# A recurrent mixer with both directions' gates and scans merged, on one core of Trainium2

## The chip, the cores and the metric

The kernel runs on one core of a Trainium2 chip. The core has four compute engines with a queue of their own each: TensorE (PE; its weight loads are listed as PEld), VectorE (DVE), ScalarE (ACT) and GpSimd (POOL). A fifth, SyncE (SP), issues most of the DMA transfers. Each queue is worked off in order, and engines wait for each other by semaphores. The metric is the device time of one execution in microseconds, as the median of the runs.

## The reference

Two layers work on 256 latent tokens and 256 context tokens of width 1024, in fp32. Layer 0 is differential attention and a SwiGLU. Layer 1 is a gated linear recurrence in two directions (the part that is changed) and a mixture of eight experts of which each token takes two. Cut to the recurrence:

```python
def rglru_coeffs(u, w_gates, b_gates, a_param):
    ...
    g = jax.nn.sigmoid(g.astype(jnp.float32))
    r_t, i_t = g[0], g[1]
    log_a = RG_C * r_t * jax.nn.log_sigmoid(a_param.astype(jnp.float32))
    a_t = jnp.exp(log_a)
    b_t = jnp.sqrt(-jnp.expm1(2.0 * log_a)) * (i_t * u.astype(jnp.float32))
    return a_t, b_t

def rglru_mixer(...):
    gate_l = jax.nn.gelu(proj_l[..., :D_RNN])
    u_l = depthwise_conv(proj_l[..., D_RNN:], conv_w, conv_b)
    u_c = depthwise_conv(proj_c[..., D_RNN:], conv_w, conv_b)
    for d, reverse in enumerate((False, True)):
        a_c, b_c = rglru_coeffs(u_c, gate_w[d], gate_b[d], a_param[d])
        h_c = linear_scan(a_c, b_c, h0, reverse)
        h_c_final = h_c[:, 0] if reverse else h_c[:, -1]
        a_l, b_l = rglru_coeffs(u_l, gate_w[d], gate_b[d], a_param[d])
        lat_states.append(linear_scan(a_l, b_l, h_c_final, reverse))
    y_l = ((lat_states[0] + lat_states[1]) * gate_l) @ w_out
```

The context is scanned first and hands its last state to the scan of the latents. Behind it come the residual, a norm, the router and the experts.

## The kernel before, in words

Channels lie on the 128 partitions, so the 1024 channels are eight blocks `b` of 128 x 512 (256 latents, then 256 context tokens). Most products are made in three passes: a weight is split into a rounded half (`split_hi`, a cast on ScalarE, line 148) and a rest (`split_lo`, a subtraction on VectorE or GpSimd, line 152). `hi(key)` and `lo(key)` do that for the two halves of one load.

For each block the recurrence goes through these steps:
- `u_proj(b)` on TensorE: 24 products into a PSUM bank; `gate_proj(g)` makes the gate of two blocks, whose copy (line 1235) is on ScalarE.
- `conv(b)`: four VectorE operations (lines 1255 to 1258) from that bank into `u`.
- `gate_mm(b)`: four TensorE products `lg` (line 1265), two gates for each direction.
- `gates(b)` on ScalarE: for each direction Sigmoids into `r_t` and `i_t` (line 1274) and a Tanh into `t_t` (line 1275).
- `exps(b, own)` on ScalarE: `a = exp(...)` in place of `r_t` (line 1289) and its square into `a2`, which is another Exp (line 1288), or for directions under `own` a GpSimd product (line 1291).
- `in_gate(b)`: `i_t` times `u` (line 1279); on GpSimd for blocks 2, 6 and 7, else on VectorE. `one_less(b)` on VectorE: `(a2 + 1) * t_t` (line 1298). `roots(b)` on ScalarE: a square root of that (line 1302). All of these are done once for each direction.
- `scans(b)` on VectorE: for each direction a product (line 1308) and two scans (lines 1311 to 1317), then the sum of both directions into `YS` (line 1320). `times_gate(k0, k1)` multiplies `YS` by the gate (line 1328).

`r_t`, `i_t` and `t_t` exist four times, so `gates(4)` waits until `scans(0)` has read its tiles. ScalarE loads a table whenever it changes between Sigmoid and Tanh, Exp, Sqrt and Gelu. VectorE, ScalarE, TensorE, GpSimd and SyncE run this part in the order in which the lines 1423 to 1536 stand, an order written out by hand that mixes the steps of several blocks.

Behind it TensorE makes the output projection `acc` from `YS` (`w_out_part`, line 1569): slices 0 to 3 for four output tiles, then slices 4 and 5, then, tile by tile, slices 6 and 7 (`w_out_end`), each followed by `add_out` (lines 486 and 487) on VectorE, a sum of squares on ScalarE, transposes, the router's logits and its choice of two, and the gather of the first expert's tokens (`gather_split`, lines 1385 to 1406). Six halves of the first expert's weights are split early: `first.split(2, eng)` for GpSimd, VectorE, GpSimd (line 1583). The rest is split as the experts run, six halves ahead of TensorE (`splits_due`). The experts' weights, 1 MB a tile, go into buffers that come free as tiles of the recurrence are done and later as weights are used.

Of the kernel before, what the change touches and what calls it, by code (L numbers as in the profile page):

```python
# [9 lines left out]
F32 = mybir.dt.float32  # L10
F32R = mybir.dt.float32r
I32 = mybir.dt.int32
AF = mybir.ActivationFunctionType
OP = mybir.AluOpType
# [3 lines left out]
P = 128  # L18
D = 1024
KD = D // P  # L20
SEQ = 256
CTX = 256
NTOK = SEQ + CTX
# [68 lines left out]
V_CB = V_CW + 32  # L92
# [6 lines left out]
def body(tc, nc, cst, rope, vec, lamv, modb, fing, x, ctx, w_m0, w_mod, w_q, w_k, w_v, w_o,  # L99
         w_gu, w_dn, w_u, w_g, w_lg, w_lo, w_rt, m_gu, m_dn, out):  # L100
    mm = nc.tensor.matmul
    V, A, G = nc.vector, nc.scalar, nc.gpsimd
# [235 lines left out]
    vc = persist.tile([P, V_N], F32, name="vc")  # L338
# [159 lines left out]
    st = pool(name="start", bufs=2)  # L498
# [88 lines left out]
    with tc.manual_schedule(engines={ENG.PE, ENG.DVE, ENG.Activation, ENG.Pool}):  # L587
# [93 lines left out]
        ls = persist.tile([P, 3, 16], F32, name="ls")  # L681
# [251 lines left out]
    with tc.manual_schedule(engines={ENG.PE, ENG.DVE, ENG.Activation, ENG.Pool}):  # L933
# [9 lines left out]
        for u in range(NH * 4):  # L943
# [9 lines left out]
            if wT:  # L953
                pv(*wT)
                if qt == 0:
                    root, scale = head_norm(hd - 1)
# [30 lines left out]
        root, scale = head_norm(NH - 1)  # L987
# [155 lines left out]
    for half in range(2):  # L1143
        FHt = fp.tile([P, FH, NTOK], F32R, name="FHt", bufs=1)
        FLt = fp.tile([P, FH, NTOK], F32R, name="FLt", bufs=1)
        first = 0
        if half == 0:

            first = 2
# [73 lines left out]
    blk = {}  # L1223
# [19 lines left out]
    def u_proj(b, c0=0, c1=NTOK):  # L1243

        w, j = wus[b // 2], b % 2
        if b not in blk:
            blk[b] = {"u": US[b] if b < 4 else lru_u.tile([P, NTOK], F32, name="U"), "ps": bank("u")}
        for k in range(KD):
            mm3(blk[b]["ps"][:, c0:c1], w(k, j * P, (j + 1) * P), (hH[:, k, c0:c1], hL[:, k, c0:c1]),
                start=(k == 0), stop=(k == KD - 1))  # L1250

    def conv(b):
        u, ps = [t.rearrange("p (s t) -> p s t", s=2) for t in (blk[b]["u"], blk[b]["ps"])]
        cw = [vc[:, V_CW + q * 8 + b:V_CW + q * 8 + b + 1] for q in range(4)]
        V.tensor_scalar(u, ps, cw[2], vc[:, V_CB + b:V_CB + b + 1], op0=OP.mult, op1=OP.add)
        V.scalar_tensor_tensor(u[:, :, 2:], ps[:, :, :SEQ - 2], cw[0], u[:, :, 2:], op0=OP.mult, op1=OP.add)
        V.scalar_tensor_tensor(u[:, :, 1:], ps[:, :, :SEQ - 1], cw[1], u[:, :, 1:], op0=OP.mult, op1=OP.add)
        V.scalar_tensor_tensor(u[:, :, :SEQ - 1], ps[:, :, 1:], cw[3], u[:, :, :SEQ - 1],
                               op0=OP.mult, op1=OP.add)

    def gate_mm(b):
        blk[b]["lg"] = []
        for ds in range(4):
            ps = bank("lg")
            mm(ps, wlg[b // 4][:, b % 4, ds], blk[b]["u"], start=True, stop=True)  # L1265
            blk[b]["lg"].append(ps)

    def gates(b):
        r, it, tt = [lru.tile([P, 2, NTOK], F32, name=n, tag=f"{n}{b % 4}", bufs=1) for n in ("r_t", "i_t", "t_t")]
        blk[b].update(r=r, i=it, t=tt)  # L1270
        for d in range(2):
            for s in range(2):
                col = V_GB + (2 * d + s) * 8 + b
                A.activation((r, it)[s][:, d], blk[b]["lg"][2 * d + s], AF.Sigmoid, bias=vc[:, col:col + 1])
            A.activation(tt[:, d], r[:, d], AF.Tanh, scale=ls[:, 2, d * 8 + b:d * 8 + b + 1])

    def in_gate(b, eng=G):
        for d in range(2):
            eng.tensor_tensor(blk[b]["i"][:, d], blk[b]["i"][:, d], blk[b]["u"], op=OP.mult)

    def exps(b, own):

        r = blk[b]["r"]
        blk[b]["a2"] = []
        for d in range(2):
            a2 = lru.tile([P, NTOK], F32, name="a2", bufs=3)
            if d >= own:
                A.activation(a2, r[:, d], AF.Exp, scale=ls[:, 1, d * 8 + b:d * 8 + b + 1])
            A.activation(r[:, d], r[:, d], AF.Exp, scale=ls[:, 0, d * 8 + b:d * 8 + b + 1])
            if d < own:  # L1290
                G.tensor_tensor(a2, r[:, d], r[:, d], op=OP.mult)
            blk[b]["a2"].append(a2)

    def one_less(b):

        tt = blk[b]["t"]
        for d in range(2):
            V.scalar_tensor_tensor(tt[:, d], blk[b]["a2"][d], 1.0, tt[:, d], op0=OP.add, op1=OP.mult)

    def roots(b):  # L1300
        for d in range(2):
            A.activation(blk[b]["t"][:, d], blk[b]["t"][:, d], AF.Sqrt)

    def scans(b):
        st = []
        for d in range(2):
            aa, bv = blk[b]["r"][:, d], blk[b]["i"][:, d]
            V.tensor_mul(bv, bv, blk[b]["t"][:, d])
            s = lr2.tile([P, NTOK], F32, name=f"st{d}")
            if d == 0:  # L1310
                V.tensor_tensor_scan(s[:, SEQ:], aa[:, SEQ:], bv[:, SEQ:], 0.0, op0=OP.mult, op1=OP.add)
                V.tensor_tensor_scan(s[:, :SEQ], aa[:, :SEQ], bv[:, :SEQ], s[:, NTOK - 1:NTOK],
                                     op0=OP.mult, op1=OP.add)
            else:
                V.tensor_tensor_scan(s[:, :SEQ - 1:-1], aa[:, :SEQ - 1:-1], bv[:, :SEQ - 1:-1], 0.0,
                                     op0=OP.mult, op1=OP.add)
                V.tensor_tensor_scan(s[:, SEQ - 1::-1], aa[:, SEQ - 1::-1], bv[:, SEQ - 1::-1],
                                     s[:, SEQ:SEQ + 1], op0=OP.mult, op1=OP.add)
            st.append(s)
        V.tensor_add(YS[:, b], st[0][:, :SEQ], st[1][:, :SEQ])  # L1320
# [5 lines left out]
    def times_gate(k0, k1):  # L1326
        y, gt = [t[:, k0:k1].rearrange("p k n -> p (k n)") for t in (YS, GT)]
        V.tensor_mul(y, y, gt)
# [87 lines left out]
    with tc.manual_schedule(engines={ENG.PE, ENG.DVE, ENG.Activation, ENG.Pool, ENG.SP}):  # L1416
# [41 lines left out]
        gate_mm(2)  # L1458
        lo(("g", 1))
        exps(0, 0)  # L1460
        in_gate(0, V)
        u_proj(3)
        one_less(1)
        conv(3)
# [6 lines left out]
        one_less(2)  # L1471
        roots(0)
        load_u(3)
        in_gate(1, V)
        conv(4)
        roots(2)
        gate_mm(3)
# [17 lines left out]
        scans(1)  # L1495
        gate_mm(5)
        gates(5)
        in_gate(3, V)
        lo(("g", 3))
        exps(5, 1)  # L1500
        one_less(3)
# [5 lines left out]
        gate_proj(3)()  # L1507
        gelu(0, 8)
        one_less(5)
        scans(3)  # L1510
        roots(5)
        roots(4)
        u_proj(7)
        times_gate(0, 4)
        conv(7)
        gate_mm(6)
        in_gate(4, V)
        gate_mm(7)
        in_gate(5, V)
        scans(4)  # L1520
        gates(6)
        gates(7)
        exps(6, 0)
        scans(5)
        one_less(6)
        exps(7, 1)
        one_less(7)
        times_gate(4, 6)
        in_gate(6)
        roots(7)  # L1530
        roots(6)
        scans(6)
        in_gate(7)
        scans(7)
        times_gate(6, 7)
        times_gate(7, 8)
        close(lru_u)
        close(lru)
# [28 lines left out]
        def w_out_part(t, dh, ks):  # L1567
            for kk in ks:
                mm(acc[t, dh], YS[:, kk, t * P:(t + 1) * P], ws[dh, kk // 4][:, kk % 4], start=(kk == 0),
                   stop=(kk == KD - 1))  # L1570
# [9 lines left out]
        for tag in ("whi", "wlo"):  # L1580
            halves.put(tag, [hip.tile([P, 1024], F32R, name=tag, tag=tag) for _ in range(HL)])
        mem["hi"] = halves
        for eng in (G, V, G):
            first.split(2, eng)
        for t in range(2):
            for kk in range(4, 6):
                for dh in range(2):
                    w_out_part(t, dh, [kk])

# [56 lines left out]
            V.scalar_tensor_tensor(key[:, t], rk[:, t * NE:(t + 1) * NE], 1.0, mask[:, t], op0=OP.add, op1=OP.mult)  # L1646

        def w_out_end(t, dh):
            w_out_part(t, dh, range(6, KD))
            add_out(rt, acc[t, dh], G1b, t, dh)  # L1650

        w_out_end(0, 0)
# [528 lines left out]
```

## Time and profile before

| | |
|---|---|
| median of 3 runs | 1687.04 us (1685.44 to 1689.09) |
| the profiled execution | 1685.75 us, its span 1683.9 us |
| TensorE busy | 1636.5 us, 97% of the span |
| VectorE, ScalarE, GpSimd busy | 1100.8, 794.3, 61.3 us |
| from the first cast for the recurrence's third load to the last gating product | 679 to 798 us |
| first product of the experts | 818 us |

A profiled execution lists every instruction with its start (us from the start of the span) and length, and in brackets how long its engine had been idle before it and which instruction ended that. Busy time of TensorE is no measure of need, since its matmuls overlap; idle time of an engine matters only where that engine is the one the others wait for. The changed lines lie between 668 and 830 us, some 10% of the span. Everything behind runs in an order that the change leaves alone.

### The profile page before, as it was taken

To read this page: it belongs to the slowest core of one execution; us is meant where nothing else is said; L and a number is where in the kernel's file an instruction comes from. 1 tells how busy PE (TensorE), PEld (TensorE's weight loads), DVE (VectorE), ACT (ScalarE), POOL (GpSimd) and SP (SyncE) were. 2 spreads that over 40 slices of the span, in tenths; PEclk is the share of its full clock that TensorE was granted. 3 is DMA by queue.
4 is the path that set the end of the run, shared out by engine and by line. 5 is a ranking of instruction groups with operands and counts; after the bars stand their busy time and mean duration, and the time that the engine had idled before them with its cause. 6 is when DMAs were issued, how large, how long until landed. Compare 5 with 4: busy or idle time off the path is not lost.

```text
span 1683.9 us, 21275 instructions
## 1 busy us (share of the span) xinstructions
PE 1636.5 (97%) x7878; PEld 1154.3 (69%) x7878; DVE 1100.8 (65%) x1595; ACT 794.3 (47%) x1194; POOL 61.3 (4%) x62
## 2 busy tenths in 40 slices
PE   8999999999999999996999999999999999999996
PEld 6877788888788878772777656566565665656642
DVE  5578887967675735799797567465675665655522
ACT  4366674422122324894675455344554444544411
POOL 0001110000000001114000000000000000000000
PEclk9999999999999999998999999999999999999998
DMA  9333313545664622235888999999999999999994
GB/s 381 114 151 150 151 51 129 209 178 181 237 255 133 246 90 94 90 146 196 327 321 347 374 417 420 421 417 404 417 420 421 419 404 418 420 420 419 403 420 202
DMA packets 75488, 480.35 MB, mean 285 GB/s; under 512 B 14284, under 2 KB 14924, under 8 KB 18920
## 3 DMA queue, kind: packets, MB, share of 16 engines
q1 hardware_dynamic: 66976, 474.38, 70.5%
q10 hardware_dynamic: 8392, 4.45, 1.1%
q8 instruction: 66, 1.08, 0.3%
q14 instruction: 54, 0.44, 0.1%
HBM read 477.70 MB, written 1.10 MB: 284 GB/s over the span
## 4 chain that ended last, share of the span: by engine, by line
PE 91%; DVE 6%; ACT 1%; issue 1%; DMA 0%; POOL 0%; ACTq 0%; SPq 0%; POOLq 0%; DVEq 0%
PE b L1829 12%; PE b L332 9%; PE b L333 9%; PE b L334 9%; PE b L1880 6%; PE gu L332 5%; PE gu L333 5%; PE gu L334 5%; PE dacc L332 2%; PE dacc L333 2%; PE dacc L334 2%; PE b L1374 2%; PE p L334 1%; PE p L332 1%; PE p L333 1%; PE lg L1265 1%
## 5 line engine op out<-in xcount | busy, mean ns | idle before, releaser
L152 DVE TENSOR_TENSOR wlo<-raw,whi 128x1024 fp32r<-128x1024 f32 x341 | 405.8, 1216 | 114.0 <-ACT whi L148 112.7
L148 ACT CAST whi<-raw 128x1024 fp32r<-128x1024 f32 x346 | 352.7, 1044 | 221.2 <-PE b L333 63.8
L332 PE MATMUL b<-whi,xH 128*128 128x512 f32 x448 | 181.9, 406 | 1.2 <-ACT xH L1402 1.2
L1829 PE MATMUL b<-raw,xF 128*64 128x512 f32 x592 | 180.9, 594 | 0.0
L334 PE MATMUL b<-wlo,xH 128*128 128x512 f32 x448 | 177.6, 396 | 2.1 <-DVE wlo L152 2.1
L333 PE MATMUL b<-whi,xL 128*128 128x512 f32 x448 | 177.7, 397 | 0.0
L332 PE MATMUL gu<-hH,whi 128*128 128x512 f32 (+1 forms) x384 | 143.0, 372 | 0.0
L334 PE MATMUL gu<-hL,whi 128*128 128x512 f32 (+1 forms) x384 | 142.6, 371 | 0.0
L333 PE MATMUL gu<-hH,wlo 128*128 128x512 f32 (+1 forms) x384 | 142.6, 371 | 0.0
L152 DVE TENSOR_TENSOR wlo<-mraw,whi 128x1024 fp32r<-128x1024 f32 x106 | 126.6, 1222 | 23.4 <-ACT whi L148 23.1
L148 ACT CAST whi<-mraw 128x1024 fp32r<-128x1024 f32 x106 | 108.1, 1049 | 34.0 <-PE b L333 32.5
L1829 PE MATMUL b<-mraw,xF 128*64 128x512 f32 x304 | 118.2, 595 | 0.0
L1846 ACT ACTIVATE sges<-b 128x256 f32<-128x256 f32 x28 | 10.7, 384 | 223.0 <-PE b L1829 223.0
L1829 PEld LDWEIGHTS b<-raw,xF 128*64 128x64 f32 x592 | 55.8, 137 | 87.4 <-issue 84.1
L332 PEld LDWEIGHTS b<-whi,xH 128*128 128x128 f32 x448 | 84.3, 188 | 36.1 <-issue 16.1
L1847 DVE TENSOR_TENSOR sges<-sges,b 128x256 f32<-128x256 f32 x28 | 11.8, 421 | 145.3 <-ACT sges L1846 145.3
L1106 DVE SCALAR_TENSOR_TENSOR mac<-raw,SC,mac 128x512 f32<-128x512 f32 x140 | 98.2, 749 | 4.1 <-DMA raw<-w_mod 3.2
L334 PEld LDWEIGHTS b<-wlo,xH 128*128 128x128 f32 x448 | 84.3, 188 | 23.0 <-DVE wlo L152 2.6
L333 PEld LDWEIGHTS b<-whi,xL 128*128 128x128 f32 x448 | 84.4, 188 | 19.0 <-DVE xL L1403 0.5
L1880 PE MATMUL b<-raw,aF 128*64 128x512 f32 x352 | 91.2, 598 | 0.5 <-ACT aF L1858 0.5
L332 PE MATMUL b<-whi,aH 128*128 128x512 f32 x224 | 89.0, 397 | 0.0
L333 PE MATMUL b<-whi,aL 128*128 128x512 f32 x224 | 88.4, 395 | 0.0
(350 smaller groups left out, 2954.3 us busy)
## 6 DMA issues: line engine op xcount, KB each, us to landing
raw<-m_gu SPq DMA_DIRECT2D x147, 1024.0 KB
raw<-m_dn SPq DMA_DIRECT2D x86, 1024.0 KB
mraw<-m_gu SPq DMA_DIRECT2D x77, 1024.0 KB
raw<-w_mod SPq DMA_DIRECT2D x40, 1024.0 KB
mraw<-m_dn SPq DMA_DIRECT2D x26, 1024.0 KB
raw<-w_gu SPq DMA_DIRECT2D x22, 1024.0 KB
mw<-w_m SPq DMA_DIRECT2D x8, 1024.0 KB
raw<-w_dn SPq DMA_DIRECT2D x8, 1024.0 KB
```

The lines of the kernel that those rows point to most:

```text
L148: A.copy(h["hi"][:, :h["w"]], h["src"])
L152: eng.tensor_tensor(h["lo"][:, :h["w"]], h["src"], h["hi"][:, :h["w"]].bitcast(F32), op=OP.subtract)
L332: mm(ps, lh, rh, start=start, stop=False)
L333: mm(ps, ll, rh, start=False, stop=False)
L334: mm(ps, lh, rl, start=False, stop=stop)
L1106: V.scalar_tensor_tensor(ac[:, q], w[:, j], SC[:, k, m:m + 1], ac[:, q], op0=OP.mult, op1=OP.add)
L1265: mm(ps, wlg[b // 4][:, b % 4, ds], blk[b]["u"], start=True, stop=True)
L1374: mm(ps, XN[:, t, k * P:(k + 1) * P], oh[:, t, 0:ps.shape[-1]], start=(t == 0 and n == 0), stop=(t == 1 and n == per - 1))
L1829: mm(gu[0][64 * h:64 * h + 64], xF[:, kk], w, start=(kk == 0), stop=(kk == KD - 1), tile_position=(0, 64 * h), skip_group_check=True)
L1846: A.activation(part, ps[:, 0:256], AF.Silu)
L1847: V.tensor_mul(part, part, ps[:, 256:512])
L1880: mm(E[i]["y"][64 * dh:64 * dh + 64], lhs, w, start=(c == 0 and j == 0), stop=(c == EC - 1 and j == 3), tile_position=(0, 64 * dh), skip_g ...
```

## The change

- `conv`: the first of its four operations goes to ScalarE, as an Identity with scale and bias.
- `in_gate`, `one_less`, `roots` and the product in `scans` work on both directions in one instruction of 128 x 1024. `in_gate` is on VectorE for every block. The scans write in place of `i_t`. `a2` is two tiles of double size instead of three.
- Order: `u_proj(7)`, `conv(7)`, `gate_mm(6)` and `gate_mm(7)` go ahead of `scans(3)`; both `gates(6)` and `gates(7)` go ahead of `scans(4)`, `exps(7, 1)` ahead of `scans(5)`; `in_gate(6)` and `in_gate(7)` stand between `one_less(6)` and `scans(6)`; `times_gate(6, 7)` goes ahead of `scans(7)`.
- Four halves of the experts' weights are split early, all four on GpSimd, instead of six.
- Slice 6 of the output projection is multiplied along with slices 4 and 5; `w_out_end` only does slice 7.

```diff
-        V.tensor_scalar(u, ps, cw[2], vc[:, V_CB + b:V_CB + b + 1], op0=OP.mult, op1=OP.add)
+        A.activation(u, ps, AF.Identity, scale=cw[2], bias=vc[:, V_CB + b:V_CB + b + 1])
...
-    def in_gate(b, eng=G):
+    def in_gate(b):
+        it, u = blk[b]["i"], blk[b]["u"]
+        V.tensor_tensor(it, it, u[:, None].to_broadcast([P, 2, NTOK]), op=OP.mult)
+
+    def exps(b, own):
+
+        r = blk[b]["r"]
+        a2 = blk[b]["a2"] = lru.tile([P, 2, NTOK], F32, name="a2", bufs=2)
         for d in range(2):
-            eng.tensor_tensor(blk[b]["i"][:, d], blk[b]["i"][:, d], blk[b]["u"], op=OP.mult)
...
         tt = blk[b]["t"]
-        for d in range(2):
-            V.scalar_tensor_tensor(tt[:, d], blk[b]["a2"][d], 1.0, tt[:, d], op0=OP.add, op1=OP.mult)
+        V.scalar_tensor_tensor(tt, blk[b]["a2"], 1.0, tt, op0=OP.add, op1=OP.mult)
 
     def roots(b):
-        for d in range(2):
-            A.activation(blk[b]["t"][:, d], blk[b]["t"][:, d], AF.Sqrt)
+        A.activation(blk[b]["t"], blk[b]["t"], AF.Sqrt)
 
     def scans(b):
         st = []
+        V.tensor_mul(blk[b]["i"], blk[b]["i"], blk[b]["t"])
         for d in range(2):
             aa, bv = blk[b]["r"][:, d], blk[b]["i"][:, d]
-            V.tensor_mul(bv, bv, blk[b]["t"][:, d])
-            s = lr2.tile([P, NTOK], F32, name=f"st{d}")
+            s = bv
...
         one_less(5)
-        scans(3)
+        u_proj(7)
+        conv(7)
         roots(5)
         roots(4)
-        u_proj(7)
+        gate_mm(6)
+        gate_mm(7)
+        scans(3)
         times_gate(0, 4)
-        conv(7)
-        gate_mm(6)
-        in_gate(4, V)
-        gate_mm(7)
-        in_gate(5, V)
-        scans(4)
+        in_gate(4)
+        in_gate(5)
         gates(6)
         gates(7)
+        scans(4)
         exps(6, 0)
+        exps(7, 1)
         scans(5)
         one_less(6)
-        exps(7, 1)
+        in_gate(6)
         one_less(7)
+        roots(6)
+        roots(7)
         times_gate(4, 6)
-        in_gate(6)
-        roots(7)
-        roots(6)
+        in_gate(7)
         scans(6)
-        in_gate(7)
+        times_gate(6, 7)
         scans(7)
-        times_gate(6, 7)
         times_gate(7, 8)
...
-        for eng in (G, V, G):
-            first.split(2, eng)
-        for t in range(2):
-            for kk in range(4, 6):
+        first.split(4, G)
+        for kk in range(4, 7):
+            for t in range(2):
                 for dh in range(2):
                     w_out_part(t, dh, [kk])
...
-            w_out_part(t, dh, range(6, KD))
+            w_out_part(t, dh, [KD - 1])
```

## Rows read from the trace of the kernel before

**Rows 1.** The page, chain of work that ended last, by engine

```profile
PE 91%; DVE 6%; ACT 1%; issue 1%; DMA 0%; POOL 0%; ACTq 0%; SPq 0%; POOLq 0%; DVEq 0%
```

**Rows 2.** By stretch: us, busy us and instructions, granted clock, DMA share, GB/s

```profile
690.00:720.00 30.00, 30.00 (x129) 21.73 (x128) 21.74 (x26) 29.75 (x43) 5.01 (x4) 1.00 0.31 108
721.60:798.20 76.60, 59.36 (x228) 36.46 (x227) 74.89 (x90) 53.61 (x71) 23.11 (x13) 0.93 0.44 165
...
1000.00:1100.00 100.00, 100.00 (x467) 62.72 (x464) 60.27 (x69) 45.48 (x57) 0.00 (x0) 1.00 1.01 421
```

**Rows 3.** Timeline 676 to 690 (start, us, engine, line): ScalarE, then VectorE

```profile
679.24 1.05 ACT L148 CAST whi<-raw 128x1024 fp32r<-128x1024 f32 x1 [2.72 <-issue]
...
681.71 1.28 ACT L1274 ACT_TABLE_LOAD   x1
686.96 0.69 ACT L1274 ACTIVATE r_t<-lg,vc 128x512 f32<-128x512 f32 x1 [3.97 <-PE lg L1265]
...
686.10 0.81 DVE L1255 TENSOR_SCALAR U<-u,vc 128x512 f32<-128x512 f32 x1 [2.11 <-PE u L334]
```

**Rows 4.** Timeline of ScalarE, 667 and 716 to 723

```profile
667.09 1.11 ACT L461 ACTIVATE tp<-tp,sh,gs 128x256 f32<-128x256 f32 x2 [2.43 <-PE tp L447]
...
716.63 0.69 ACT L1274 ACTIVATE r_t<-lg,vc 128x512 f32<-128x512 f32 x1
...
722.51 2.02 ACT L148 CAST whi<-raw 128x1024 fp32r<-128x1024 f32 x2
```

**Rows 5.** Timeline of VectorE, 712 to 723

```profile
712.03 1.28 DVE L1279 TENSOR_TENSOR i_t<-i_t,U 128x512 f32<-128x512 f32 x2
...
718.58 0.81 DVE L1255 TENSOR_SCALAR U<-u,vc 128x512 f32<-128x512 f32 x1
719.42 0.75 DVE L1256 SCALAR_TENSOR_TENSOR U<-u,vc,U 128x508 f32<-128x508 f32 x1
...
721.65 0.68 DVE L1308 TENSOR_TENSOR i_t<-i_t,t_t 128x512 f32<-128x512 f32 x1
722.37 0.69 DVE L1311 TENSOR_TENSOR_SCAN st<-r_t,i_t 128x256 f32<-128x256 f32 x1
```

**Rows 6.** Timeline 768 to 794: VectorE, then GpSimd

```profile
771.91 6.56 DVE L1298 SCALAR_TENSOR_TENSOR t_t<-a,t_t 128x512 f32<-128x512 f32 x4
...
784.11 2.78 DVE L1308 TENSOR_TENSOR i_t<-i_t,t_t 128x512 f32<-128x512 f32 x1
...
772.85 6.75 POOL L1279 TENSOR_TENSOR i_t<-i_t,U 128x512 f32<-128x512 f32 x4
781.19 10.58 POOL L152 TENSOR_TENSOR wlo<-raw,whi 128x1024 fp32r<-128x1024 f32 x4 [1.59 <-ACT whi L148]
```

**Rows 7.** Timeline 735 to 803: VectorE, then TensorE

```profile
735.91 2.35 DVE L152 TENSOR_TENSOR wlo<-raw,whi 128x1024 fp32r<-128x1024 f32 x2
...
739.79 0.28 PE L332 MATMUL gp<-hH,whi 128*128 128x256 f32 x1
...
751.01 3.60 PE L1265 MATMUL lg<-U,wlg 128*128 128x512 f32 x8
760.39 5.13 PE L1265 MATMUL lg<-U,wlg 128*128 128x512 f32 x8 [5.78 <-DVE U L1258]
...
797.84 5.19 PE L1569 MATMUL acc<-wlo,YS 128*128 128x512 f32 x8 [10.51 <-DVE YS L1328]
```

**Rows 8.** Timeline 797 to 818: VectorE, ScalarE, TensorE

```profile
797.37 0.75 DVE L1328 TENSOR_TENSOR YS<-YS,GT 128x256 f32<-128x256 f32 x2
...
801.36 0.69 DVE L486 TENSOR_TENSOR xadd<-acc,G1b 128x512 f32<-128x512 f32 x1 [0.96 <-PE acc L1569]
...
808.19 0.69 DVE L487 TENSOR_TENSOR XL<-XL,xadd 128x512 f32<-128x512 f32 x1
...
816.46 0.89 ACT L1394 ACTIVATE gath<-gath,sh,gs 128x128 f32<-128x128 f32 x2 [4.75 <-PE gath L1374]
...
817.96 0.48 PE L332 MATMUL b<-whi,xH 128*128 128x512 f32 x1
```

More of the change, by code (lines that the diff above doesn't have):

```diff
@@ L1275, in gates @@
             A.activation(tt[:, d], r[:, d], AF.Tanh, scale=ls[:, 2, d * 8 + b:d * 8 + b + 1])
-    def in_gate(b, eng=G):
-        for d in range(2):
-            eng.tensor_tensor(blk[b]["i"][:, d], blk[b]["i"][:, d], blk[b]["u"], op=OP.mult)
+    def in_gate(b):
+        it, u = blk[b]["i"], blk[b]["u"]
+        V.tensor_tensor(it, it, u[:, None].to_broadcast([P, 2, NTOK]), op=OP.mult)
     def exps(b, own):
         r = blk[b]["r"]
-        blk[b]["a2"] = []
+        a2 = blk[b]["a2"] = lru.tile([P, 2, NTOK], F32, name="a2", bufs=2)
         for d in range(2):
-            a2 = lru.tile([P, NTOK], F32, name="a2", bufs=3)
             if d >= own:
-                A.activation(a2, r[:, d], AF.Exp, scale=ls[:, 1, d * 8 + b:d * 8 + b + 1])
+                A.activation(a2[:, d], r[:, d], AF.Exp, scale=ls[:, 1, d * 8 + b:d * 8 + b + 1])
             A.activation(r[:, d], r[:, d], AF.Exp, scale=ls[:, 0, d * 8 + b:d * 8 + b + 1])
             if d < own:
-                G.tensor_tensor(a2, r[:, d], r[:, d], op=OP.mult)
-            blk[b]["a2"].append(a2)
+                G.tensor_tensor(a2[:, d], r[:, d], r[:, d], op=OP.mult)
     def one_less(b):
         tt = blk[b]["t"]
-        for d in range(2):
-            V.scalar_tensor_tensor(tt[:, d], blk[b]["a2"][d], 1.0, tt[:, d], op0=OP.add, op1=OP.mult)
+        V.scalar_tensor_tensor(tt, blk[b]["a2"], 1.0, tt, op0=OP.add, op1=OP.mult)
     def roots(b):
-        for d in range(2):
-            A.activation(blk[b]["t"][:, d], blk[b]["t"][:, d], AF.Sqrt)
+        A.activation(blk[b]["t"], blk[b]["t"], AF.Sqrt)
     def scans(b):
         st = []
+        V.tensor_mul(blk[b]["i"], blk[b]["i"], blk[b]["t"])
         for d in range(2):
             aa, bv = blk[b]["r"][:, d], blk[b]["i"][:, d]
-            V.tensor_mul(bv, bv, blk[b]["t"][:, d])
-            s = lr2.tile([P, NTOK], F32, name=f"st{d}")
+            s = bv
             if d == 0:
@@ L1460, in body @@
         exps(0, 0)
-        in_gate(0, V)
+        in_gate(0)
         u_proj(3)
@@ L1473, in body @@
         load_u(3)
-        in_gate(1, V)
+        in_gate(1)
         conv(4)
@@ L1497, in body @@
         gates(5)
-        in_gate(3, V)
+        in_gate(3)
         lo(("g", 3))
```

## The prediction

> **What bounds the kernel now.** I read the page first: the chain that ended last is 91% TensorE and 6% VectorE [rows 1]. The 6% is what an edit of the recurrence can reach, so the next view is the table by stretch [rows 2]. From 690 to 720 us TensorE is busy 30.00 of 30 us and ScalarE 29.75: ScalarE has no slack there, while VectorE has 8 us. From 721.6 to 798.2 it is the other way round: VectorE is busy 74.89 of 76.6 us, which is back to back but for the gaps between dependent instructions, and TensorE only 59.36. So one loop runs through both: ScalarE sets the pace until the first scans, VectorE from there to the last gating product, which ends at 798.1 [rows 8]. TensorE then finishes the output projection, the router and the gather, and the experts' first product starts at 817.96 [rows 8]. From 1000 to 1100 us the DMA share is 1.01 [rows 2], so the loads run without a pause there. What shifts the start of the experts shifts the buffers that their loads wait for, so I carry a shift of 817.96 to the end one to one. The question is where 817.96 goes.
>
> **The change, part by part.**
>
> (a) *ScalarE's queue up to the first scans.* The first operation of `conv` moves from VectorE to ScalarE. There it stands in program order: `conv(2)` (line 1450) is ahead of the casts `hi(("u", 2))` (line 1452), which are ahead of `gates(0)`. Before, ScalarE made the first of those two casts at 679.24, loaded the table at 681.71, and then sat idle 3.97 us until the gates' products came at 686.96 [rows 3]. After, the first of these is the operation of `conv(2)`, which waits for `u_proj(2)`; VectorE's row of the same step has it start at 686.10, released by that product [rows 3]. Nothing behind it on ScalarE can use the idle time. Its price: the trace shows no such instruction on 512 columns. The nearest rows are the Sigmoid from PSUM on 512 columns, 0.69 us [rows 3], and Identity on 256 columns, 1.11 us for two [rows 4], so 0.55 each; the same step on VectorE took 0.81 [rows 5]. I take 0.69 with 0.1 of it overlapped by the next, because size and source are the same, and keep 0.55 to 0.81. So `gates(0)` starts at 686.1 + 0.6 + two casts of 0.95 + a load of 1.3 = 689.9, late by 2.9 us. ScalarE has no slack in 690 to 720 to win this back, and takes on two more such operations (`conv(3)`, `conv(4)`): 1.2 us more, less 0.2 for square roots done in three calls rather than six. `gates(3)` goes from 716.63 [rows 4] to 720.5. Behind it, in order, stand two casts and the copy of the gate projection, and only then the operation of `conv(5)`. From 716.63 to the end of that copy's slot at 722.51 are 5.9 us, so it runs at 726.4 to 727.1. VectorE stands still for it, although it could have gone on at 719.42 as before; the three other operations of `conv(5)` follow (719.42 to 721.65, 2.2 us [rows 5]), and `scans(0)` starts at 729.4 rather than 721.65: **7.7 us late**. VectorE's relief up to here is worth nothing; it only waits longer.
>
> One sentence of the Trainium skill bears on this price without entering it: the page "ScalarE: Activation LUTs", section "Table sets: the hidden batching unit", says that identity is in every table set. The trace agrees as far as it goes, since Identity at 667.09 runs with no load in front [rows 4], but no row shows it between Sigmoids or Exps. Were it not so, each of these operations could cost two loads of 1.28 us, and ScalarE would be later still.
>
> (b) *VectorE from the first scans to the last.* It works without a break, so instructions are counted.
> - First operation of `conv(6)` and `conv(7)` gone: 2 x 0.84 (718.58 to 719.42 [rows 5]) = -1.7.
> - The scans' two products in one: a 128x512 one holds its successor up by 0.72 (721.65 to 722.37 [rows 5]); a subtraction on 128x1024 lasts 1.22 (two in 2.35 [rows 7]), or 1.26 with the gap; -0.18 each, eight times: -1.4.
> - `in_gate(3)` to `in_gate(5)` and `one_less(3)` to `one_less(7)`: a pair takes 1.28 [rows 5], one of double size 1.22; -0.05 each: -0.4.
> - `in_gate(6)` and `in_gate(7)` come over from GpSimd: 2 x 1.15 = +2.3.
> - With that GpSimd's four products go, and so does their hold on VectorE. Beside them four `one_less` took 6.56 us [rows 6], against 2.4 at the pair's pace [rows 5]. -4.1 (a square of `exps(7, 1)` on GpSimd stays, and holds VectorE as now).
> - GpSimd's four weight splits stay as many. Their place in the code is behind `roots`, and what releases them is the cast on ScalarE, not the scans; the first starts some 2 us behind `one_less(7)`, so beside `scans(6)` as now. One of them and one operation of VectorE alternate: 10.58 us for four, while a product of 0.68 took 2.78 [rows 6]. Longer operations of VectorE don't change what GpSimd takes in between, about 2 us each. 0.
>
> Sum: -5.3. Against it stands a new wait. `conv(7)` now precedes `scans(3)`, and on VectorE everything queues behind it. `u_proj(7)` follows `gate_proj(3)` on TensorE, which needs the split weights of `lo(("g", 3))`. VectorE made these at 735.91, before TensorE asked at 739.79 [rows 7]; now the first is there at 735.91 + 7.7 - 0.4 + 1.2 = 744.4. TensorE idles close to 5 us. After 5.78 us of idling eight product records took 5.13 us instead of 3.60 [rows 7], so I add 1.7 for the lowered clock (0 if it holds). Projections as before 11.2 us (739.79 to 751.01 [rows 7]): 757.5, and with ScalarE's step 758.2. VectorE is there at 751.1 + 7.7 - 1.5 = 757.3. It waits about 1 us. The early `conv(7)` spares TensorE its 5.78 us wait of now, but TensorE is not what the scans wait for.
> The last gating product ends at 798.1 + 7.7 - 5.3 + 1.0 = 801.5, 3.4 us late.
>
> (c) *The tail.* Now the last two slices of the output projection are multiplied behind the scans, at the lowered clock after 10.51 us of idling: eight records in 5.19 us [rows 7]. The first addition starts at 801.36, 3.2 us behind the last gating product, and the last ends at 808.88 [rows 8], with VectorE waiting for TensorE in between. After, slice 6 is multiplied during `scans(7)` and raises the clock again, and slice 7 needs one matmul per tile: the first addition starts 1.3 us behind (-1.9), and four additions of 1.4 us with one wait for the row sums make 6.7 instead of 7.5 (-0.8). Together -2.7. Two VectorE splits (2.36 us) that now hide behind TensorE's slow start also go; they hid there, 0.
>
> (d) *The splits not made early.* Four halves are ready when the experts start, not six. Two casts and two subtractions move into the experts' first steps. ScalarE idles 4.75 us before the gathered tokens come [rows 8]; if they are queued there they are free, if they stand behind it they cost up to 2 x 1.15 = 2.3. I take 0.4, since their inputs and buffers are free long before.
>
> Sum: +3.4 - 2.7 + 0.4 = +1.1. The profiled execution took 1685.75 us, 1.3 under the median of 1687.04; it would become 1686.9, and the median **1688.1 us**. With the ends of the unknown prices (four operations at 0.55 or 0.81; no drop of the clock; 0 or 2.3 for the splits) the likeliest case reaches from 1686.2 to 1691.0.
>
> **The rivals.**
> *ScalarE keeps up.* If its new operations fell into idle time (the queue built in another order than the program's lines), `scans(0)` would start 0.8 us early, VectorE would meet `u_proj(7)` at 751.0 and wait 3.8 us there, and the scans would end at 798.1 - 1.7 - 5.3 + 3.8 = 794.9; with the tail and (d) -5.5: 1681.5. For it: the 3.97 us of idling [rows 3]. Against: every queue of the recurrence follows the lines of the program. 0.18.
> *The moved splits decide (slower).* If both engines take them ahead of the gathered tokens' scaling, the first product waits 2.3 us, and TensorE, idle that long, gets the lower clock, 1.7 us as in (b): 2.3 + 1.7 = 4.0 more than nothing, instead of 0.4: 1691.7. It decides from the point at which the fifth half is not split when TensorE is through four. For it: ScalarE and VectorE then have the scaling, the splits and their normal supply to do at once; against: ScalarE's idle time in front [rows 8]. 0.22.
> *GpSimd's splits really come behind the scans*, as the change's title says. Then the hold of 4 x 2 us on the last scans goes: 1680.1. The Trainium skill speaks for that order: "GPSIMD Engine Reference", section "8. Key points", says that the two engines contend where VectorE reads two SBUF inputs, as the scans do, and the rows above agree. But no wait puts the splits there. 0.06.
>
> **How the numbers follow.** Likeliest case 0.50, the rivals 0.18, 0.22 and 0.06, the rest open. A change under 0.2% (3.4 us) can't be told from none here: 1683.7 to 1690.4. Faster holds two rivals, 0.23; slower the second rival and the end of the likeliest case, 0.27; the same, 0.50. The range reaches from the first rival to beyond the second: 1681.0 to 1693.0.
>
> **What would show it.** Right: ScalarE casting for `u, 2` behind 686; VectorE idle for some 5 us in front of `conv(5)` with ScalarE as the releaser; `scans(0)` near 729; TensorE idle near 740 to 745; GpSimd's splits beside `scans(6)` with VectorE operations of 2.6 us; the first addition within 1.5 us of the last gating product. Wrong: `scans(0)` before 724, or the splits behind 800.

## The result: slower by 0.85%, and the profile after

| | before | after |
|---|---|---|
| median | 1687.14 us | 1702.58 us (1699.70 to 1703.08) |
| ratio | 1 | 1.0085, 95% interval 1.0073 to 1.0097 |
| span of the profiled execution | 1683.9 us | 1697.8 us |
| `scans(0)` starts | 721.65 | 729.54 (forecast 729.4) |
| last gating product ends | 798.12 | 803.23 (forecast 801.5) |
| first addition starts | 801.36 | 814.25 (forecast 802.8) |
| first product of the experts | 817.96 | 831.95 |

The forecast was 1688.1 in a range of 1681.0 to 1693.0: wrong by some 14 us. The table already says where to look. The first half of the recurrence came out as forecast, the second half within 2 us, and then VectorE did nothing for 11 us in front of the first addition. From there on the distance to before stays what it is: 14.0 us at the experts' start, 13.9 in the span.

The first forecast steps can be read off five rows of ScalarE and VectorE, which answer to [rows 3 to 5] (start, length, engine, line, tiles, then idle time before and its releaser):

```profile
686.17 0.78 ACT L1255 ACTIVATE U<-u,vc 128x512 f32<-128x512 f32 x1 [4.69 <-PE u L334]
...
690.14 0.69 ACT L1274 ACTIVATE r_t<-lg,vc 128x512 f32<-128x512 f32 x1
...
720.60 0.69 ACT L1274 ACTIVATE r_t<-lg,vc 128x512 f32<-128x512 f32 x1
...
726.47 0.81 ACT L1255 ACTIVATE U<-u,vc 128x512 f32<-128x512 f32 x1
...
727.31 0.75 DVE L1256 SCALAR_TENSOR_TENSOR U<-u,vc,U 128x508 f32<-128x508 f32 x1 [5.31 <-ACT U L1255]
```

ScalarE stands 4.69 us in front of `conv(2)`, reaches `gates(0)` at 690.14 (forecast 689.9), `gates(3)` at 720.60 (720.5) and the operation of `conv(5)` at 726.47 (726.4). VectorE waits 5.31 us for that. No such wait was there before.

A later stop agrees in its size but not in its cause. VectorE waits 0.79 us in front of `conv(7)` (forecast about 1), for ScalarE. ScalarE's operation was to wait for `u_proj(7)` at TensorE's lowered clock. But the last product of `u_proj(7)` (line 334) starts at 756.22, and ScalarE gets there only at 757.45, right behind its Gelu (line 1320), which the forecast hadn't counted. The rows are ScalarE's and TensorE's of after; below them stands ScalarE's in *late_splits*, a kernel of the next section, where it does wait for TensorE:

```profile
755.63 1.92 ACT L1320 ACTIVATE GT<-GT 128x2048 f32<-128x2048 f32 x1
757.45 0.76 ACT L1255 ACTIVATE U<-u,vc 128x512 f32<-128x512 f32 x1
...
756.22 0.39 PE L334 MATMUL u<-hL,whi 128*128 128x512 f32 x1
```

```profile
757.63 0.78 ACT L1255 ACTIVATE U<-u,vc 128x512 f32<-128x512 f32 x1 [0.21 <-PE u L334]
```

Now the end of the recurrence. These are VectorE's rows of after from `scans(7)` on (line 1302 is the merged product, 1307 to 1313 the scans, 1324 the gating product, 486 the first addition):

```profile
796.20 1.22 DVE L1302 TENSOR_TENSOR i_t<-i_t,t_t 128x1024 f32<-128x1024 f32 x1
797.34 1.22 DVE L152 TENSOR_TENSOR wlo<-raw,whi 128x1024 fp32r<-128x1024 f32 x1
798.47 0.68 DVE L1307 TENSOR_TENSOR_SCAN i_t<-r_t,i_t 128x256 f32<-128x256 f32 x1
799.07 1.20 DVE L152 TENSOR_TENSOR wlo<-raw,whi 128x1024 fp32r<-128x1024 f32 x1
800.19 0.74 DVE L1308 TENSOR_TENSOR_SCAN i_t<-r_t,i_t 128x256 f32<-128x256 f32 x1
...
802.80 0.43 DVE L1324 TENSOR_TENSOR YS<-YS,GT 128x256 f32<-128x256 f32 x1
814.25 0.69 DVE L486 TENSOR_TENSOR xadd<-acc,G1b 128x512 f32<-128x512 f32 x1 [11.02 <-DMA G1b<-mrows]
```

Two things here stand in no forecast. Two weight splits (line 152) lie between the operations of `scans(7)`, where they delay the last gating product by 1.13 and 1.12 us. And the first addition waits 11.02 us for a transfer: `G1b`, the row of gates that `add_out` multiplies by. The chain of waits that ended last says why, piece by piece (start, length, what):

```profile
797.42 1.14 DVE wlo L152
798.55 0.60 DVE i_t L1307
799.15 1.13 DVE wlo L152
800.30 0.33 SPq L135
800.73 0.38 SPq L135
801.20 0.38 SPq L135
801.63 0.65 SPq L135
802.33 11.82 DMA G1b<-mrows
814.25 0.70 DVE xadd L486
```

The second split releases SyncE, which then issues four weight loads (line 135) and only then `G1b`, whose transfer lands 11.82 us later. The next two rows are SyncE's issue of `G1b`, in before and in after. The third is from SyncE's waits between 700 and 835 us of after (us in total, times, the longest):

```profile
778.54 0.33 SPq L1564 DMA_DIRECT2D G1b<-mrows  x1
```

```profile
802.33 0.44 SPq L1560 DMA_DIRECT2D G1b<-mrows  x1
```

```profile
SPq L135 <- DVE wlo L152: 75.9, 4, 41.6
```

For 41.6 us SyncE stood in front of one load. The load is for the buffer from which the two late splits read: `split` frees a buffer with every second half and at once orders the next load into it. Six early splits stood among the lines of the recurrence, so that load came behind `G1b`. With four, the last two halves of the third buffer are split by the experts' code instead. Its lines keep an order of their own on VectorE, and SyncE's order isn't laid down there at all (the recurrence's block names SP among the engines whose order is fixed, the experts' block doesn't). In the program that was built, the two splits are placed inside `scans(7)` and the load stands ahead of three other weight loads and of `G1b`. SyncE's queue is worked off in order, so all of them wait for a split that has nothing to do with them.

### The profile page after: what moved, and what is told of

It reads as the page before. It is cut to its first block, busy times and chain, and to the rows that moved or that the text cites. A ratio compares the mean times of both kernels' runs of the same rounds, so it can differ in the third digit from the quotient of the medians.

```text
span 1697.8 us, 21243 instructions
## 1 busy us (share of the span) xinstructions
PE 1642.0 (97%) x7878; PEld 1156.0 (68%) x7878; DVE 1089.3 (64%) x1569; ACT 798.5 (47%) x1194; POOL 54.5 (3%) x56
## 4 chain that ended last, share of the span: by engine, by line
PE 90%; DVE 5%; ACT 3%; DMA 1%; issue 1%; POOL 0%; SPq 0%; ACTq 0%; POOLq 0%; DVEq 0%
PE b L1824 11%; PE b L332 9%; PE b L333 9%; PE b L334 9%; PE b L1875 6%; PE gu L332 5%; PE gu L333 5%; PE gu L334 5%; PE dacc L332 2%; PE dacc L333 2%; PE dacc L334 2%; PE b L1370 2%; PE p L334 1%; PE p L332 1%; PE p L333 1%; PE lg L1265 1%
## 5 line engine op out<-in xcount | busy, mean ns | idle before, releaser
L152 DVE TENSOR_TENSOR wlo<-raw,whi 128x1024 fp32r<-128x1024 f32 x345 | 412.1, 1220 | 116.1 <-ACT whi L148 115.3
L148 ACT CAST whi<-raw 128x1024 fp32r<-128x1024 f32 x350 | 356.7, 1044 | 222.1 <-PE b L333 67.3
L152 DVE TENSOR_TENSOR wlo<-mraw,whi 128x1024 fp32r<-128x1024 f32 x102 | 121.8, 1222 | 21.7 <-ACT whi L148 21.0
L148 ACT CAST whi<-mraw 128x1024 fp32r<-128x1024 f32 x102 | 103.9, 1048 | 31.9 <-PE b L333 30.8
L1824 PE MATMUL b<-mraw,xF 128*64 128x512 f32 x296 | 114.2, 594 | 0.0
L334 PE MATMUL b<-wlo,aH 128*128 128x512 f32 x224 | 88.4, 395 | 0.0
```

The lines of the kernel that those rows point to most:

```text
L148: A.copy(h["hi"][:, :h["w"]], h["src"])
L152: eng.tensor_tensor(h["lo"][:, :h["w"]], h["src"], h["hi"][:, :h["w"]].bitcast(F32), op=OP.subtract)
L334: mm(ps, lh, rl, start=False, stop=stop)
L1824: mm(gu[0][64 * h:64 * h + 64], xF[:, kk], w, start=(kk == 0), stop=(kk == KD - 1), tile_position=(0, 64 * h), skip_group_check=True)
```

## The experiments

Times between executions shift by up to 2 us before the changed lines are reached. So milestones are counted from the same event in each: the start of the first operation of `conv(2)`, set to 686.10 as in before. Each column is the difference to before; the last is the span.

| kernel | `scans(0)` | last gating product | first addition | experts' first product | end |
|---|---|---|---|---|---|
| after | +7.8 | +5.0 | +12.8 | +13.9 | +13.8 |
| six_splits | +7.8 | +4.3 | +3.2 | +2.8 | +1.0 |
| g1b_ahead | +7.8 | +5.4 | +6.2 | +5.7 | +5.7 |
| four_splits_alone | 0.0 | +2.1 | +11.1 | +13.2 | +13.3 |
| late_splits | +7.8 | +3.4 | +1.7 | +2.2 | +2.3 |
| conv_scalar_alone | +8.1 | +6.5 | +6.9 | +6.9 | +6.9 |
| six_splits_conv_vector | -2.3 | -3.0 | -4.1 | -4.6 | -6.2 |
| late_splits_conv_vector | -2.3 | -3.1 | -4.6 | -4.1 | -4.1 |
| gpsimd_behind_scans | -2.3 | -11.0 | -12.0 | -3.6 | -12.4 |
| tile_alone | -2.3 | -3.1 | -4.3 | -0.8 | -10.6 |
| behind_scans_no_tile | -2.3 | -11.0 | -12.0 | -4.3 | -4.0 |
| before_with_tile | 0.0 | +0.5 | +0.8 | +1.8 | -8.0 |
| no_gpsimd_splits | -2.3 | -11.0 | -12.0 | -12.5 | -21.2 |

### Is it the queue?

*six_splits*, the changed kernel with its six early splits back:

```diff
-        first.split(4, G)
+        for eng in (G, V, G):
+            first.split(2, eng)
```

> The changed kernel with its six early splits put back (GpSimd two, VectorE two, GpSimd two). Theory (queue): in the changed kernel the two halves left to the experts' steps are what puts a weight load ahead of G1b in SyncE's queue; with them back in the recurrence's own order G1b is issued before 785, the first addition no longer waits for its transfer, GpSimd holds the last scans with two splits fewer, and the first addition starts near 800 (814.25 in the changed kernel): about 1688 to 1690 us. Rival (tiles): the scans in place and the larger a2 make the experts' buffers come free later; then the wait for G1b stays some 10 us and the time 1700 to 1703.

Measured 1687.72 us, 0.9998 of before (0.9988 to 1.0007), at the low end of what was expected. The theory holds, the rival (tiles) falls.

```profile
782.26 0.33 SPq L1560 DMA_DIRECT2D G1b<-mrows  x1
```

```profile
803.97 2.35 DVE L152 TENSOR_TENSOR wlo<-raw,whi 128x1024 fp32r<-128x1024 f32 x2
806.25 0.68 DVE L486 TENSOR_TENSOR xadd<-acc,G1b 128x512 f32<-128x512 f32 x1
```

`G1b` is issued at 782.26 and nobody waits for it. One part of what I expected was wrong: GpSimd makes four splits in either kernel, so the scans are held as before, and the first addition came at 804.6 in the table's count, not near 800. VectorE's two splits fill the 2.2 us between the last gating product and the addition.

*g1b_ahead* leaves the queue as it is and moves `G1b` one place up in it:

```diff
-        first.add(places(mrawL[:3]))
         G1b = mo.tile([P, 1, D], F32, name="G1b", tag="G")
         nc.sync.dma_start(G1b[:, 0], mrows[3, 0:1, :].to_broadcast([P, D]))
+        first.add(places(mrawL[:3]))
```

> The changed kernel with the load of G1b one place further ahead: in front of the three weight loads that stood before it, but still behind the load that waits for the late splits. Theory (queue, and then 4 MB of weights ahead of it on the DMA engines): G1b is still issued only at 800.7, but has 1 MB in front of it rather than 4; it lands near 805, the first addition starts near 806, and the time is about 1694. Rival (only the late issue counts, the transfer itself takes some 11 us wherever it stands): first addition near 812, 1700 to 1701.

Measured 1693.26 us, 1.0033 (1.0022 to 1.0045). SyncE's row, then VectorE's:

```profile
802.59 0.38 SPq L1559 DMA_DIRECT2D G1b<-mrows  x1
```

```profile
809.10 0.69 DVE L486 TENSOR_TENSOR xadd<-acc,G1b 128x512 f32<-128x512 f32 x1 [4.01 <-DMA G1b<-mrows]
```

Issued as late as in after, `G1b` is used 6.5 us later instead of 11.9, and the wait falls from 11.02 to 4.01. So the wait has two parts: SyncE's late issue, and the weights that were issued first and are still being moved (three of the four megabytes are gone here). This run also rules out the late weight loads themselves as the cause: they start as late as in after, yet the end is 5.7 us behind before, exactly as the experts' start.

*four_splits_alone*, the kernel before with this one part of the change:

```diff
-        for eng in (G, V, G):
-            first.split(2, eng)
+        first.split(4, G)
```

> The kernel before with one part of the change alone: four early splits on GpSimd instead of six on both engines. Theory (queue): the last two halves are split by VectorE inside scans(7), some 2.3 us, the load into their buffer goes ahead of G1b on SyncE's queue, G1b is issued near 799 and lands near 811, and the first addition starts there rather than at 801.4: about 1697. Rival (the moved splits cost what the prediction gave them, 0.4, or 4 at most): 1687.5 to 1691.

Measured 1699.16 us, 1.0072 (1.0055 to 1.0088). VectorE waits as in after:

```profile
812.22 0.69 DVE L486 TENSOR_TENSOR xadd<-acc,G1b 128x512 f32<-128x512 f32 x1 [12.22 <-DMA G1b<-mrows]
```

One line of the change, on its own, costs most of what the whole change costs: 0.72% against 0.85%, and 13.3 us against 13.8 in the profiled executions. The others come to nothing together, as *six_splits* showed (0.9998). *late_splits* is the changed kernel with the two halves split by VectorE behind the additions, in the order of the recurrence:

```diff
         w_out_end(1, 1)
+        first.split(2)
```

> The changed kernel, with the two halves that it leaves to the experts' steps split by VectorE behind the four additions instead, in the recurrence's own order. G1b is then issued early and nothing stands between the last gating product and the first addition: this is the kernel that the prediction thought it had. Theory (everything but the queue was right): last gating product some 3 to 4.3 us later than before, counted from the start of conv(2), first addition 1.3 us behind it, first product of the experts 1.5 to 2.5 us late: 1687 to 1689 us, no change from before. Rival (the tail gains nothing, because VectorE's two splits only move to where the router waits): first product 4 us late, 1691.

Measured 1689.72 us, 1.0016 (1.0006 to 1.0025), a little more than expected. This is the kernel that the prediction worked out, and its steps can be compared one by one:

```profile
801.00 0.42 DVE L1324 TENSOR_TENSOR YS<-YS,GT 128x256 f32<-128x256 f32 x1
802.98 0.69 DVE L486 TENSOR_TENSOR xadd<-acc,G1b 128x512 f32<-128x512 f32 x1 [1.55 <-PE acc L1565]
...
810.31 2.36 DVE L152 TENSOR_TENSOR wlo<-raw,whi 128x1024 fp32r<-128x1024 f32 x2 [0.55 <-ACT whi L148]
```

The last gating product is 3.4 us late (forecast 3.4), the first addition 1.56 us behind it (1.3), the additions end 1.0 us late (3.4 - 2.7 = 0.7). Another 1.3 us are lost from there to the experts, where the two splits now stand.

### What does ScalarE's share cost?

*conv_scalar_alone*, the kernel before with this part alone:

```diff
-        V.tensor_scalar(u, ps, cw[2], vc[:, V_CB + b:V_CB + b + 1], op0=OP.mult, op1=OP.add)
+        A.activation(u, ps, AF.Identity, scale=cw[2], bias=vc[:, V_CB + b:V_CB + b + 1])
```

> The kernel before with one part of the change alone: the first operation of conv on ScalarE. Theory (the prediction's step a): ScalarE stands in front of conv(2) until u_proj(2) is done, scans(0) start near 729 instead of 721.65, VectorE wins back 1.7 in conv(6) and conv(7), and the time is about 1693. Rival (ScalarE keeps up): scans(0) near 721 and 1685.5.

Measured 1694.12 us, 1.0035 (1.0020 to 1.0049), as expected; VectorE waits 5.50 us in front of `conv(5)`, and `scans(0)` starts 8.1 us late. *six_splits_conv_vector* undoes it in the kernel with six splits:

```diff
-        A.activation(u, ps, AF.Identity, scale=cw[2], bias=vc[:, V_CB + b:V_CB + b + 1])
+        V.tensor_scalar(u, ps, cw[2], vc[:, V_CB + b:V_CB + b + 1], op0=OP.mult, op1=OP.add)
```

> The changed kernel with its six early splits and the first operation of conv back on VectorE. Theory (ScalarE's order costs the 7.8 us at scans(0), and VectorE's merges are worth 5): scans(0) near 721 again, last gating product some 2 us earlier than before, first addition 2.2 us behind it: about 1684. Rival (VectorE bounds it all the same, and eight operations of 0.84 come back): about the 1687.7 of the same kernel with conv on ScalarE.

Measured 1681.02 us, 0.9963 (0.9949 to 0.9977), 3 us less than expected. With the operation on VectorE, the rest of the change is a gain: the scans start 2.3 us early and end 3.0 us early. That is close to the prediction's first rival, which had ScalarE keep up (3.2 early at the last gating product), and its wait is there, too: VectorE meets `u_proj(7)` at 751.04 (751.0 in the rival) and has waited 3.21 us for it (3.8).

```profile
751.04 0.81 DVE L1255 TENSOR_SCALAR U<-u,vc 128x512 f32<-128x512 f32 x1 [3.21 <-PE u L334]
```

*late_splits_conv_vector* is *late_splits* with the same edit:

> The changed kernel with two splits behind the additions and the first operation of conv back on VectorE. Theory: as the kernel with six splits and conv on VectorE, less the 0.9 us by which the first addition comes nearer to the last gating product: about 1683. Rival: no gain over the six splits.

Measured 1681.46 us, 0.9968 (0.9956 to 0.9981): no gain over the six splits, as its rival said. The first addition comes half a microsecond nearer, and the splits take it back on the router's path.

### GpSimd behind the scans, and a surprise

*gpsimd_behind_scans* builds the prediction's third rival, on top of *late_splits_conv_vector*: GpSimd first reads the last sum of `scans(7)`, so that its splits come behind the scans.

```diff
+        behind = mo.tile([P, 1], F32, name="behind")
+        G.tensor_tensor(behind, YS[:, 7, 0:1], YS[:, 7, 0:1], op=OP.mult)
         first.split(4, G)
```

> As the kernel with two splits behind the additions and conv on VectorE, and GpSimd's four splits made to wait for the last sum of scans(7) by a small GpSimd product that reads it. This makes the change's title true. Theory (the prediction's third rival: four splits hold four scans by 2 us each): scans of 0.7 us throughout, last gating product 8 us earlier than with the splits beside them; but the splits now stand beside the additions, which they can hold by 2 us each as they held the scans, so that between none and all of the 8 us stays: 1675 to 1683. If the additions, which read one operand from PSUM, are not held, it is at the low end.

Measured 1673.54 us, 0.9913 (0.9896 to 0.9930), some 1.5 us below the range expected, and not for the reason given. GpSimd's row and VectorE's:

```profile
787.27 10.17 POOL L152 TENSOR_TENSOR wlo<-raw,whi 128x1024 fp32r<-128x1024 f32 x4
```

```profile
783.19 0.69 DVE L1307 TENSOR_TENSOR_SCAN i_t<-r_t,i_t 128x256 f32<-128x256 f32 x1
...
789.17 0.69 DVE L486 TENSOR_TENSOR xadd<-acc,G1b 128x512 f32<-128x512 f32 x1 [2.21 <-PE acc L1565]
789.89 2.57 DVE L487 TENSOR_TENSOR XL<-XL,xadd 128x512 f32<-128x512 f32 x1
792.57 0.69 DVE L486 TENSOR_TENSOR xadd<-acc,G1b 128x512 f32<-128x512 f32 x1
793.29 1.93 DVE L487 TENSOR_TENSOR XL<-XL,xadd 128x512 f32<-128x512 f32 x1
```

The scans are free (0.69 us; beside the splits 2.6 to 2.8), and the last gating product is 11.0 us early, 7.9 more than without the wait: the prediction's price of 4 x 2 us was right. But the hold moved on to the additions. Of their two operations the one that reads PSUM keeps its 0.69 us, the one with both inputs in SBUF takes up to 2.57. The Trainium skill ("GPSIMD Engine Reference", section "8. Key points") names two SBUF inputs on VectorE as one of two conditions under which the engines contend; these rows agree. The last addition ends 9.1 us early. TensorE then makes the router's products at the lower clock. The row of the stretch 800 to 810 (us; busy us and instructions of PE, PEld, DVE, ACT, POOL; granted clock; DMA share; GB/s) reads 0.50, the lower level of 1.2 GHz:

```profile
800.00:810.00 10.00, 10.00 (x48) 10.00 (x48) 5.76 (x19) 4.92 (x9) 0.55 (x1) 0.50 0.69 272
```

Of 11.0 us only 3.6 arrive at the experts. And yet the end is 12.4 us early. The missing 8.8 us come in over the experts, bit by bit, where products follow each other more closely. Two kernels tell the order of the splits from the new tile. *tile_alone* has the tile, written behind the additions, and the splits as in *late_splits_conv_vector*; *behind_scans_no_tile* writes a spare column of an old tile instead. Their edits, the first against *late_splits_conv_vector*, the second against *gpsimd_behind_scans*:

```diff
+        behind = mo.tile([P, 1], F32, name="behind")
         first.split(4, G)
...
         w_out_end(1, 1)
+        G.tensor_tensor(behind, XL[:, 0, 1023:1024], XL[:, 0, 1023:1024], op=OP.mult)
         first.split(2)
```

```diff
-        behind = mo.tile([P, 1], F32, name="behind")
-        G.tensor_tensor(behind, YS[:, 7, 0:1], YS[:, 7, 0:1], op=OP.mult)
+        G.tensor_tensor(mhalf[:, 7:8], YS[:, 7, 0:1], YS[:, 7, 0:1], op=OP.mult)
```

> The kernel with two splits behind the additions and conv on VectorE, with the one-column tile of the kernel 'GpSimd behind the scans' but not its order: the tile is allocated in the same place, so that the tokens' tiles behind it lie 32 bytes further on, and the small GpSimd product that writes it stands behind the additions, where nothing waits for it. In the kernel 'GpSimd behind the scans' the experts' products followed each other after 0.227 us, in the others after 0.233, and 8.7 of its 14.5 us came evenly over the experts, from 3.7 us ahead of before at the first expert to 12.4 at the end. Theory (place of the tiles): the same spacing here, and 8 to 9 us less than the 1681.5 of the same kernel without the tile: about 1673. Rival (order of the splits): 0.233 us and 1681.5.

> As 'GpSimd behind the scans', but the small product that holds GpSimd's splits back writes a spare column of a tile that exists anyway, so no tile is moved. Theory (place of the tiles): the last gating product again 11 us and the first product of the experts 3.5 us ahead of before, the experts' products 0.233 us apart, and no more gained behind: 1681 to 1685. Rival (order of the splits): 0.227 us apart and 1673.5.

Measured 1673.09 us (0.9910; 0.9893 to 0.9926) with the tile alone, 1681.73 us (0.9962; 0.9949 to 0.9974) with the order alone. So the order is worth nothing at the end (1681.46 without it), and the tile 8.4 us. (In the profiled execution of *tile_alone* the experts start only 0.8 us early, because the granted clock was 0.51 from 810 to 815, where it was 1.00 without the tile.) *before_with_tile* puts the same two lines (the tile and the product that writes it) into the kernel before and nothing else:

> The kernel before with the one-column tile alone, written behind the additions, and no other part of the change. Theory (place of the tiles): products 0.227 us apart through the experts, 8 to 9 us less: about 1679, a gain over before with no step of the change in it. Rival (the spacing belongs to the changed recurrence): 1688.

Measured 1677.38 us, 0.9941 (0.9924 to 0.9957). Of eight products in a row of an expert, the first and the last, in before and then in *tile_alone*:

```profile
839.62 0.39 PE L333 MATMUL b<-whi,xL 128*128 128x512 f32 x1
...
841.25 0.40 PE L334 MATMUL b<-wlo,xH 128*128 128x512 f32 x1
```

```profile
839.61 0.39 PE L333 MATMUL b<-whi,xL 128*128 128x512 f32 x1
...
841.20 0.39 PE L334 MATMUL b<-wlo,xH 128*128 128x512 f32 x1
```

Seven steps take 1.63 us in one, 0.233 each, and 1.59 in the other, 0.227. The experts make 3 x 448 + 3 x 224 = 2016 such products (counts of the page of after), some 12 us at that difference; 9.8 arrive in both kernels with the tile alone, changes of the clock included.

### A version that beats both

*no_gpsimd_splits* takes what the others left. All six casts go first; VectorE makes two subtractions ahead of the first addition and four while it waits for the gathered tokens:

```diff
-        first.split(4, G)
+        behind = mo.tile([P, 1], F32, name="behind")
+        for h in first.halves[:6]:
+            split_hi(h)
...
+        early_lo(2)
         w_out_end(0, 0)
...
         place_of(oh, key, 0, 1)
+        early_lo(4)
```

(`early_lo` does the rest of `split` on VectorE; `conv` is on VectorE as before; the product that writes `behind` stands where *tile_alone* has it.)

> The changed kernel with the first operation of conv back on VectorE, the one-column tile, and no early split on GpSimd: all six casts on ScalarE as before, two subtractions on VectorE between the last gating product and the first addition, four in the gap in which VectorE waits for the gathered tokens (3.3 us long, four take 4.6). Theory: last gating product 11 us ahead of before as in 'GpSimd behind the scans', additions not held, first product of the experts 10 to 11 us ahead, and 8.7 more from the place of the tiles: 1667 to 1670. Rival (VectorE has no room for four splits there, or TensorE meets the experts at the lower clock after idling): first product 4 to 7 us ahead, 1672 to 1676.

Measured 1665.84 us, 0.9866 (0.9850 to 0.9883): 21.7 us less than before, and a little less than expected.

```profile
788.55 2.35 DVE L152 TENSOR_TENSOR wlo<-raw,whi 128x1024 fp32r<-128x1024 f32 x2
790.85 0.69 DVE L486 TENSOR_TENSOR xadd<-acc,G1b 128x512 f32<-128x512 f32 x1
791.58 0.69 DVE L487 TENSOR_TENSOR XL<-XL,xadd 128x512 f32<-128x512 f32 x1
...
803.41 4.62 DVE L152 TENSOR_TENSOR wlo<-raw,whi 128x1024 fp32r<-128x1024 f32 x4
```

VectorE makes a split in 1.15 us; on GpSimd each one took 2 us from VectorE anyway. Nothing is held, and all 12 us reach the experts. The other 8.7 us come over the experts, where this kernel has the tile as well.

## Why the prediction was wrong, point by point

- **(a) ScalarE's queue: right.** 7.7 us forecast, 7.8 measured, each stop on the way within 0.3 us. The unknown price, taken as 0.69 with 0.1 of overlap, was 0.78 with a successor 0.68 later. No table load stood in front of an Identity, not even between two square roots at 716.62. That is as the Trainium skill ("ScalarE: Activation LUTs", section "Table sets: the hidden batching unit") has it, where identity is in every set.
- **(b) VectorE's work: right, but for two instructions.** TensorE idled 3.49 us in front of `gate_proj(3)`'s second half (forecast close to 5). From `scans(0)` to the last gating product VectorE took 2.8 us less than before where 4.3 were forecast; the two splits inside `scans(7)` cost 2.25, without them it is 5.0. In *late_splits* the last gating product is late by the 3.4 us of the forecast. That the wait of `conv(7)` came out at 0.79 us (1.0) is luck in after: the clock stayed at 1.00 from 745 to 755, and ScalarE's Gelu made the wait. In *late_splits* the clock was 0.66 from 745 to 750, and the wait for TensorE was 1.12 us, so there the step held. Its working is slightly off: 744.4 + 11.2 + 1.7 is 757.3 and not 757.5, and the two rows that it quotes for the clock differ by 1.53 and not 1.7.
- **(c) The tail: right in its own terms,** as *late_splits* shows, but it started from the belief that the first addition has only TensorE to wait for.
- **(d) The splits not made early: this is the step that failed.** "Two casts and two subtractions move into the experts' first steps" was taken from the order of the lines, priced at 0.4 and bounded by 2.3. They went into `scans(7)` instead (2.25), and their third instruction was forgotten: the load that every second `split` issues. It stood for 41.6 us in SyncE's queue, ahead of `G1b`, and the first addition waited 11.02 us, where it waits 1.55 in *late_splits*. The text counted the casts and subtractions of the moved step, but not its transfer, nor the queue past which that moved.
- **The second rival** ("the moved splits decide") named the right edit with the wrong mechanism. It expected the first product of the experts to wait for them; TensorE never did. Its 4.0 us were too few by 9: *four_splits_alone* ends 13.3 us late.
- **"One to one to the end" held** for every kernel within 1.8 us, except where the tile changed the pace of the experts themselves. The remaining steps of 1.7 us are TensorE's clock. Near 854 TensorE waits 2.14 us for a split weight in before and in *six_splits*. Behind that wait the granted clock was 0.83 in before (850 to 860) and products were 0.43 us apart for 3 us; in *six_splits* it was 1.00 (855 to 865) and they stayed 0.23 apart. *late_splits* gains the same there and loses 1.7 us near 1330, at 0.89 against 1.00, so that its end is as late as its experts' start.
- **The first rival** has 0.8 us in its text and 1.7 in its sum for the start of the scans. The wait behind it takes up the difference, so its 794.9 stands. (In the chances, 0.18 and 0.06 make 0.24, not 0.23.)
- **The third rival** priced GpSimd's hold rightly, 7.9 us at the last gating product, but let it end there. It goes where the splits go, and the additions are on the path too.

## What to carry to other kernels

Of a step that is moved, list every instruction it issues, the transfer that refills its buffer included, and ask for each queue what may now stand behind it. A small transfer that a short, critical stretch needs should not share an in-order queue with loads that wait for far-off work (that follows from the runs; none gave `G1b` a queue of its own). And where two engines contend, moving the weaker one's work out of one stretch puts the contention into the next; giving the work to the faster engine, in time that it spends waiting, removes it.

## What the runs showed that was not expected

- **The place of a tile.** A tile of one column shifts the tiles allocated behind it by 32 bytes, among them `xH` (from 85696 to 85728 in the programs built), `xL`, `aH` and `aL`, from which TensorE loads its stationary operands; the weights' halves stay where they were. Three-pass products then follow each other after 0.227 us instead of 0.233, at the same granted clock of 1.00. That is worth 8 to 10 us at the end, more than any edit of the recurrence gained in this study but the last. Why is open: no run tried other shifts, or moved one of the tiles alone.
- **The clock after equal idling.** In front of `gate_proj(3)`'s second half TensorE idled 3.49 us in after and 3.52 in *six_splits*. In the stretch 745 to 755 the granted clock was 1.00 in the one and 0.66 in the other. The last product of `u_proj(7)` started 11.5 us behind the idle time in the one and 13.5 in the other, where `conv(7)` then waited 2.02 us. Idle time of that length doesn't say which level follows.
